# Eighteen of 64 conditioning chunks on TensorE, all of them beside w_in and w_out: a residual block on one core

## The chip, the cores and the metric

The kernel runs on one core of a Trainium2 chip. The metric is the device time of one execution in microseconds; the number for a kernel is the median of its runs. One further execution was recorded by the hardware profiler; all rows below come from it. Engines are named as the profile does: PE (TensorE), PEld (its weight loads), DVE (VectorE), ACT (ScalarE), POOL (GpSimd), SP (the queue that issues most transfers).

## The reference

One trunk layer over 256 tokens of width 2048, conditioned by a vector `c`; all in float32:

```python
mod = jax.nn.silu(c) @ w_ada[l] + b_ada[l]                     # 2048 x 12288
sh1, sc1, g1, sh2, sc2, g2 = jnp.split(mod, 6, axis=-1)
hn = rmsnorm(x) * (1.0 + sc1[:, None]) + sh1[:, None]
mix = hybrid_mixer(hn, w_in[l], ..., w_out[l])                 # 4 mLSTM heads beside 8 RG-LRU blocks
x = x + (g1[:, None] * mix).astype(x.dtype)
hn = rmsnorm(x) * (1.0 + sc2[:, None]) + sh2[:, None]
y = hier_moe(hn.reshape(B * S, D), ...)                        # 32 experts in 4 groups, 2 per token
x = x + (g2[:, None] * y).astype(x.dtype)
return rmsnorm(x) * final_g
```

The conditioning, `silu(c) @ w_ada`, is a product of one row with 96 MiB of weights. `sh1` and `sc1` are needed before `w_in`, `g1` for the first residual, `sc2` and `sh2` for the router and the experts' inputs, `g2` only where the experts' outputs are added. The router picks a group and two of its eight experts for each token.

## The kernel before, in words

All weights come in chunks of 1024 KB (128 partitions by 4 by 512 float32). SP issues the transfers in the order of the code into a ring of 7 buffers (`chunk`); a transfer waits until the chunk that had the buffer has been used. SP and PE keep the code's order, DVE and ACT are put in order by a scheduler up to the router and keep the code's order from there to the first experts (`in_order`).

**The start** (to about 140 us): the 32 chunks of `sc1` and `sh1`, on PE, with the first `w_in` chunks among them.

**Beside `w_in` and `w_out`** (to about 540 us): each of 52 chunks of `w_in` and `w_out` is split on ACT and DVE into a rounded part and a rest (`split`, lines 460 to 464, tile `ws`, three buffers of half a chunk) and multiplied on PE in three terms. After each, `between` (line 498) runs: it advances side work (gates, scores, sums) by one step and takes conditioning chunks from the generator `ada_later`. That generator has 64 chunks, 16 for each of the sections g1, sc2, sh2 and g2, in this order. A chunk goes one of two ways:

- on PE, if its number is in the set `ON_PE`: four matmuls (line 312) with the conditioning as a 32-column operand, into one PSUM tile of the section;
- on DVE else: two operations on half a chunk each (lines 320 and 322), which add to the tile `acc`.

When a section is complete, `acc_sum` (line 282) folds `acc` into the PSUM tile by four matmuls on PE, DVE adds the bias (`row`, line 289), PE turns the row into columns (line 295), and DVE writes `ada` (line 297), in `adx` too for sc2 and sh2.

`between` takes one chunk each time, and a second one at every sixth call up to the 36th. That makes 58 chunks of the 64 by the end of `w_out`. `ON_PE` holds 21 numbers, 15 of them among these 58 and the numbers 58 to 63.

**The router's wait** (about 538 to 561 us). After the last `w_out` product come the last residual (lines 782 to 784: product with the gate row `g`, addition to `X`), its transposes on PE (871), the router's product (881), and a chain of small DVE operations that ends in MS, the tokens' choices (944). PE counts them (986 to 993), DVE makes a selection matrix, and PE gathers the first round's tokens with it (970). The calls `fill(FILL[0])` and `fill(FILL[1])`, with `FILL = (4, 2)`, take four conditioning chunks behind the router's product and two behind the counting. All six are on PE.

**The experts** (to the end). Ten rounds, each with up to four experts on 32 tokens each. The chunks of the first round belong to experts 0 and 1, which need no router result (`first_weights`); they go through 13 buffers: the ring's 7, and 6 that have come free (`early`, `more`, lines 178 to 189). The later ones are addressed by the router's table `eid`. In the first round `begin` (from line 1252 on) puts the tables and one more `fill()` with `drain()` between the first chunks: there the sum of g2 is finished, and `g2_rows` spreads it.

Of the kernel before, what the change touches and what calls it, by code (L numbers as in the profile page):

```python
# [38 lines left out]
NR = len(ROUNDS)  # L39
NB = 1 + sum(n for _, n in OVER)  # L40

FILL = (4, 2)

EARLY = (2,)

BESIDE = 53


ON_PE = {0, 1, 2, 3, 5, 7, 10, 12, 14, 16, 19, 22, 32, 41, 48, 58, 59, 60, 61, 62, 63}


C_ID, C_SEL, C_LT, C_ONE, C_MASK, C_IOTA, C_SLOT = 0, 128, 176, 304, 432, 688, 817
# [54 lines left out]
def block_kernel(ctx, tc, x, c, w_ada, b_ada, w_in, b_gates, vec_a, vec_b, w_lru_a, w_lru_x, w_out,  # L107
# [20 lines left out]
    def small(shape, name):  # L128
        return st([128] + shape, name)
# [7 lines left out]
    def step():  # L137
        for q in (sums, side):
            if q:
                g = q.popleft()  # L140
                if next(g, "end") != "end":
                    q.append(g)
# [127 lines left out]
    def ada_row(sec, k):  # L270
        return chunk(w_ada[:, sec * D:sec * D + D].rearrange("(p k) (j n) -> p k j n", k=16, j=4)[:, k])
# [28 lines left out]
    def ada_later():  # L300
# [3 lines left out]
        for i, sec in enumerate((2, 4, 3, 5)):  # L304
# [3 lines left out]
            for k in range(16):  # L308
                w = ada_row(sec, k)
                if 16 * i + k in ON_PE:  # L310
                    for n in range(4):
# [184 lines left out]
    done = [0]  # L496

    def between():

        step()  # L500
        done[0] += 1
        for _ in range((done[0] < BESIDE) + (done[0] < 37 and done[0] % 6 == 0)):
            next(later, None)

    def w_in_group(col0, evac):
        ps = [pa([128, 2, S]) for _ in range(2)]
        for kk in range(4):
            by_channel(ps, kk, col0, step if col0 == 5640 else None)
            between()
        for ch in range(4):  # L510
            evac(ch, ps[ch // 2][:, ch % 2])
# [221 lines left out]
    def token_group(col0, evac):  # L733
        ps = [pa() for _ in range(2)]
        for kk in range(4):
            w = chunk(w_in[kk * 512:kk * 512 + 512, col0:col0 + 512].rearrange("(k p) n -> p k n", p=128))
            by_token(ps, w, HH, HL, kk * 4, kk == 0, kk == 3)
            between()
        for h in range(2):
            evac(h, ps[h])  # L740
# [26 lines left out]
    def w_out_chunk(ps, n, kk):  # L767
        w = chunk(w_out[kk * 512:kk * 512 + 512, n * 512:n * 512 + 512].rearrange("(k p) n -> p k n", p=128))
        Y = YM if kk < 2 else YR
        by_token(ps, w, Y[:, 0], Y[:, 1], kk % 2 * 4, kk == 2, kk == 1, step)  # L770
        between()
# [81 lines left out]
    def fill(n=1):  # L853
        for _ in range(n):
            step()
            next(later, None)
# [21 lines left out]
    for i in range(2):  # L878
        for j in range(2):
            for h in range(2):  # L880
                PE.matmul(plg[:, h], xts[i][:, j, h * 128:h * 128 + 128], wr[:, 12 + i * 2 + j], start=False,
                          stop=i == 1 and j == 1, skip_group_check=True)
    fill(FILL[0])
    for h in range(2):
        V.scalar_tensor_tensor(lg[:, h], plg[:, h], r2[:, h:h + 1], shw, op0=OP.mult, op1=OP.add)

# [104 lines left out]
        PE.matmul(pcnt[:, 0:32], ones, MS[:, h], start=h == 0, stop=h == 1)  # L991
    for h in range(2):
        PE.matmul(pcnt[:32, 32:33], MS[:, h], ones[:, 0:1], start=h == 0, stop=h == 1)
    fill(FILL[1])
    pre = small([2, 32], "pre")
    tcopy(pre, ppre)

# [333 lines left out]
```

## Time and profile before

| | us |
|---|---|
| three runs | 1353.75, 1346.56, 1346.46 |
| median of the runs | 1346.56 |
| the profiled execution, from outside | 1348.79 |
| its span in the profile | 1346.8 |
| busy in the span: PE, PEld | 1171.0, 667.1 |
| busy: DVE, ACT, POOL | 546.7, 347.9, 5.6 |

The transfers of the span are 504.81 MB, a mean of 375 GB/s. The span is what the profiler recorded between the first and the last instruction; the execution's own time is 2 us longer. Busy shares are means over stages with different limits, so they say little; what counts is read from slices and windows. A matmul's record is longer than the distance to the next one, since matmuls overlap in the array. One chunk on PE shows as eight records of line 312.

### The profile page before, as it was taken

The numbers are of one execution on the slowest core, as the hardware profiler recorded it, in microseconds if no ns is written. First come the engines' busy times: TensorE is split into PE (matmuls) and PEld (weight loads), VectorE is DVE, ScalarE is ACT, GpSimd is POOL, SyncE is SP. The second block draws the span as 40 slices with busy tenths as digits, with TensorE's granted clock in tenths as the row PEclk, the third lists the DMA queues.
The fourth block names the chain that finished last, engine by engine and source line by source line (L and its number), as shares of the span: only waits on it lengthen the run. The fifth ranks groups of instructions, "written<-read, shape, count | busy, mean of one in ns | idle before, by whom it ended". The sixth has DMA issues, their size and how long they took to land. (4 is left out here: it accounts for less than half of the span.)

```text
span 1346.8 us, 19864 instructions
## 1 busy us (share of the span) xinstructions
PE 1171.0 (87%) x8002; PEld 667.1 (50%) x8002; DVE 546.7 (41%) x987; ACT 347.9 (26%) x551; POOL 5.6 (0%) x13
## 2 busy tenths in 40 slices
PE   4898999999999999899687898878887779887885
PEld 0666889987877888443132434223341133423222
DVE  1333667779869977523013131302231013131214
ACT  2233494545445443521010011001010010101012
POOL 0000000000000000000000000000000000000000
PEclk9999999999989999899899999999998799999997
DMA  9999868689969998999999999999999999999993
GB/s 337 368 374 365 276 219 331 237 331 351 356 245 404 410 373 324 357 352 404 424 423 423 422 423 423 423 424 423 424 423 424 424 424 423 406 424 424 422 411 141
DMA packets 116896, 504.81 MB, mean 375 GB/s; under 512 B 12425, under 2 KB 14761, under 8 KB 69185
## 3 DMA queue, kind: packets, MB, share of 16 engines
q1 hardware_dynamic: 114832, 496.97, 92.5%
q0 software_dynamic: 720, 5.24, 0.9%
q8 instruction: 64, 1.05, 0.3%
q10 hardware_dynamic: 1248, 1.29, 0.3%
q14 instruction: 32, 0.25, 0.0%
HBM read 526.54 MB, written 2.10 MB: 392 GB/s over the span
## 5 line engine op out<-in xcount | busy, mean ns | idle before, releaser
L1105 PE MATMUL pa<-ring,XE 128*32 128x512 f32 x1368 | 225.8, 628 | 44.8 <-DMA ring<-in_w_e_up_dram 32.2
L463 DVE TENSOR_TENSOR ws<-ring,ws 128x1024 fp32r<-128x1024 f32 x128 | 154.9, 1221 | 64.9 <-ACT ws L462 58.5
L462 ACT ACTIVATE ws<-ring 128x1024 fp32r<-128x1024 f32 x128 | 134.7, 1060 | 164.5 <-PE pa L494 79.6
L478 PE MATMUL pa<-HH,ws 128*128 128x256 f32 x512 | 151.9, 297 | 3.6 <-ACT ws L462 1.9
L1105 PE MATMUL pa<-early,XE 128*32 128x512 f32 x656 | 135.6, 618 | 20.8 <-DMA early<-in_w_e_up_dram 12.4
L480 PE MATMUL pa<-HH,ws 128*128 128x256 f32 x512 | 149.2, 291 | 5.0 <-DVE ws L463 5.0
L479 PE MATMUL pa<-HL,ws 128*128 128x256 f32 x512 | 148.7, 290 | 1.4 <-DVE HL L373 1.4
L1105 PEld LDWEIGHTS pa<-ring,XE 128*32 128x32 f32 x1368 | 58.8, 114 | 167.9 <-issue 77.7
L1105 PE MATMUL pa<-more,XE 128*32 128x512 f32 x536 | 112.1, 616 | 15.4 <-DMA more<-in_w_e_up_dram 12.7
L1160 PE MATMUL pa<-ring,hT 128*32 128x512 f32 x640 | 108.2, 610 | 11.8 <-DMA ring<-in_w_e_down_dram 11.7
L974 ACT ACTIVATE XE<-pb,adx 128x128 f32<-128x128 f32 x80 | 36.6, 458 | 301.9 <-DVE XE L977 301.9
L478 PEld LDWEIGHTS pa<-HH,ws 128*128 128x128 f32 x512 | 102.2, 200 | 18.5 <-issue 8.4
L480 PEld LDWEIGHTS pa<-HH,ws 128*128 128x128 f32 x512 | 101.7, 199 | 6.6 <-DVE ws L463 6.6
L1137 DVE TENSOR_TENSOR hs<-hs,pa 128x512 f32<-128x512 f32 x10 | 6.9, 688 | 237.3 <-PE pa L1105 237.3
L479 PEld LDWEIGHTS pa<-HL,ws 128*128 128x128 f32 x512 | 102.1, 199 | 2.0 <-DVE HL L373 1.9
L1125 DVE TENSOR_TENSOR X<-X,pa 128x512 f32<-128x512 f32 x80 | 52.0, 684 | 116.0 <-PE pa L1123 115.9
L322 DVE SCALAR_TENSOR_TENSOR acc<-ring,cz,acc 128x1024 f32<-128x1024 f32 x78 | 98.2, 1278 | 0.4 <-DMA ring<-in_w_ada_dram 0.3
L970 PE MATMUL pb<-two,XN 128*128 128x128 f32 x640 | 77.3, 279 | 6.7 <-ACT hT L1144 6.7
L970 PEld LDWEIGHTS pb<-two,XN 128*128 128x128 f32 x640 | 73.1, 192 | 19.0 <-issue 9.2
L1105 PEld LDWEIGHTS pa<-early,XE 128*32 128x32 f32 x656 | 33.2, 113 | 83.1 <-issue 42.3
L1116 ACT ACTIVATE ys<-y 128x512 fp32r<-128x512 f32 x40 | 25.3, 632 | 181.9 <-DVE y L1114 181.9
L1160 PE MATMUL pa<-more,hT 128*32 128x512 f32 x304 | 60.7, 622 | 5.3 <-DMA more<-in_w_e_down_dram 5.3
(379 smaller groups left out, 1376.4 us busy)
## 6 DMA issues: line engine op xcount, KB each, us to landing
ring<-in_w_ada_dram SPq DMA_DIRECT2D x96, 1024.0 KB
ring<-in_w_e_gate_dram SPq DMA_DIRECT2D x62, 1024.0 KB
ring<-in_w_e_down_dram SPq DMA_DIRECT2D x61, 1024.0 KB
ring<-in_w_e_up_dram SPq DMA_DIRECT2D x57, 1024.0 KB
ring<-in_w_in_dram SPq DMA_DIRECT2D x48, 1024.0 KB
early<-in_w_e_up_dram SPq DMA_DIRECT2D x30, 1024.0 KB
more<-in_w_e_down_dram SPq DMA_DIRECT2D x29, 1024.0 KB
more<-in_w_e_up_dram SPq DMA_DIRECT2D x25, 1024.0 KB
```

The lines of the kernel that those rows point to most:

```text
L322: V.scalar_tensor_tensor(o, w[:, h:h + 2], cz[:, k, 3:4], o, op0=OP.mult, op1=OP.add)
L462: A.activation(ws[:, 0], s, AF.Copy)
L463: V.tensor_tensor(ws[:, 1], s, ws[:, 0], op=OP.subtract)
L478: PE.matmul(o, wh[:, cc], HH[:, k], start=k == 0 and ch % 2 == 0, stop=False, skip_group_check=True)
L479: PE.matmul(o, wh[:, cc], HL[:, k], start=False, stop=False, skip_group_check=True)
L480: PE.matmul(o, wl[:, cc], HH[:, k], start=False, stop=k == 15, skip_group_check=True)
L970: PE.matmul(p[:, j], XN[:, h, kk, j], which[:, h], start=h == 0, stop=h == 1)
L974: A.activation(XE[:, k], p[:, j], AF.Identity, scale=adx[:, 1, k:k + 1], bias=adx[:, 0, k:k + 1])
L1105: PE.matmul(o[c0:c0 + width], lhs(kk, j)[:, c0:c0 + width], w[:, j], start=first and j == 0, stop=last and j == 3)
L1116: A.activation(ys[0], y, AF.Copy)
L1125: V.tensor_tensor(X1[:, h, ns], X1[:, h, ns], pc, op=OP.add)
L1160: PE.matmul(pds[n][c0:c0 + width], hT[:, f, c0:c0 + width], w[:, n], start=f == 0, stop=f == 3)
```

## The change

```diff
-FILL = (4, 2)
-
-ON_PE = {0, 1, 2, 3, 5, 7, 10, 12, 14, 16, 19, 22, 32, 41, 48, 58, 59, 60, 61, 62, 63}
+ON_PE = {0, 1, 2, 3, 5, 8, 10, 13, 15, 16, 18, 20, 23, 32, 39, 48, 54, 60}
...
-        for _ in range((done[0] < BESIDE) + (done[0] < 37 and done[0] % 6 == 0)):
+        for _ in range((done[0] < BESIDE) + (done[0] < 50 and done[0] % 4 == 0)):
             next(later, None)
...
-    fill(FILL[0])
+    fill(2)
...
-    fill(FILL[1])
+    fill()
```

`between` now takes the second chunk at every fourth call up to the 48th: 52 + 12 = 64, so `ada_later` is used up by the last `w_out` chunk. Of the 64, 18 go to PE and 46 to DVE (before 21 and 43; among the 58 beside `w_in` and `w_out` 15 and 43). The calls of `fill` behind the router's product and behind the counting find no chunk and no side work left. The two lines less at the top shift every line number by two: the chunk on PE is line 310 in the changed kernel, the sum's matmuls line 280.

By groups of four `between` calls, the chunks on PE and on DVE differ in these places: the last of the RG-LRU gate's columns (4 and 0, now 4 and 1), the first k columns (2 and 2, now 3 and 2), the second v columns (0 and 4, now 1 and 4), the second o columns (1 and 4, now 0 and 5), and `w_out` in its four quarters (0 and 4, 1 and 3, 0 and 4, 0 and 4; now 1 and 4, 1 and 4, 0 and 5, 1 and 3).

On PE, from the router's transposes to the counting of the choices; before, with the four chunks of the ring between the product and the counting:

```order
L871 MATMUL pb<-cs,X_3661 128x128 x8
L881 MATMUL pa<-wr,xt 128x36 x8
L312 MATMUL pa<-ring_63,cz 32x512 x4
L312 MATMUL pa<-ring_64,cz 32x512 x4
L312 MATMUL pa<-ring_65,cz 32x512 x4
L312 MATMUL pa<-ring_66,cz 32x512 x4
L986 MATMUL pb<-MS,cs 128x32
```

and after the change, on PE from the sum of g2 to the first gather:

```order
L280 MATMUL pa<-acc,cs 32x512 x4
L293 MATMUL pb<-cs,row 128x4 x4
L869 MATMUL pb<-cs,X_3702 128x128 x8
L879 MATMUL pa<-wr,xt 128x36 x8
L984 MATMUL pb<-MS,cs 128x32
L985 MATMUL pb<-MS,cs 128x32
L986 MATMUL pb<-MS,cs 128x32
L989 MATMUL pcnt<-MS,cs 128x32 x2
L991 MATMUL pcnt<-cs,MS 32x1 x2
L968 MATMUL pb<-two,XN 128x128 x8
```

The chunks are gone from the wait, and the sum of the last section stands ahead of the router's transposes.

On DVE, the end of `w_out` and the last residual (`t` is the product with the gate, `X` the residual stream, `xt` the router's input); before:

```order
L463 TENSOR_TENSOR ws<-ring_68,ws 128x1024 x2
L322 SCALAR_TENSOR_TENSOR acc<-ring_69,cz,acc 128x1024 x2
L782 TENSOR_TENSOR t_4247<-pa,g_4202 128x512
L783 TENSOR_TENSOR X_3661<-X_3661,t_4247 128x512
L782 TENSOR_TENSOR t_4251<-pa,g_4202 128x512
L783 TENSOR_TENSOR X_3661<-X_3661,t_4251 128x512
L872 TENSOR_TENSOR xt<-pb,ada 128x512
```

and after the change:

```order
L320 SCALAR_TENSOR_TENSOR acc<-ring_68,cz,acc 128x1024 x2
L287 TENSOR_TENSOR row<-pa,brow 128x512
L780 TENSOR_TENSOR t_4283<-pa,g_4226 128x512
L295 TENSOR_SCALAR ada<-pb 128x16
L781 TENSOR_TENSOR X_3702<-X_3702,t_4283 128x512
L780 TENSOR_TENSOR t_4287<-pa,g_4226 128x512
L781 TENSOR_TENSOR X_3702<-X_3702,t_4287 128x512
L870 TENSOR_TENSOR xt<-pb,ada 128x512
```

`row`, which needs the sum's matmuls, and `ada`, which needs PE's turning of the row, stand among the operations of the residual.

On PE, in the first round of experts, where `begin` puts its tables (`eidf` and `PW`); before:

```order
L1105 MATMUL pa<-more_4560,XE 32x512 x2
L1059 MATMUL pb<-cs,eidf 1x32 x2
L1066 MATMUL pb<-cs,PW 128x128 x8
L282 MATMUL pa<-acc,cs 32x512 x4
L295 MATMUL pb<-cs,row 128x4 x4
L1105 MATMUL pa<-ring_69,XE 32x512 x2
```

and after the change:

```order
L1103 MATMUL pa<-more,XE 32x512 x2
L1103 MATMUL pa<-more_4566,XE 32x512 x2
L1057 MATMUL pb<-cs,eidf 1x32 x2
L1064 MATMUL pb<-cs,PW 128x128 x8
L1103 MATMUL pa<-ring_69,XE 32x512 x2
```

The sum is no longer there; the next expert chunk follows the tables directly.

## Rows read from the trace of the kernel before

**Rows 1.** The page, part 2: the span in 40 slices.

```profile
PE   4898999999999999899687898878887779887885
...
PEclk9999999999989999899899999999998799999997
...
GB/s 337 368 374 365 276 219 331 237 331 351 356 245 404 410 373 324 357 352 404 424 423 423 422 423 423 423 424 423 424 423 424 424 424 423 406 424 424 422 411 141
```

**Rows 2.** Windows: PE, PEld, DVE, ACT, POOL busy us, granted clock, DMA share, GB/s.

```profile
440.00:460.00 20.00, 20.00 (x96) 16.48 (x95) 19.50 (x23) 10.28 (x15) 1.05 (x2) 1.00 1.03 414
500.00:520.00 20.00, 20.00 (x106) 16.96 (x105) 17.88 (x19) 8.97 (x14) 0.00 (x0) 1.00 0.84 303
540.00:560.00 20.00, 16.93 (x116) 9.84 (x116) 10.79 (x54) 13.22 (x18) 0.00 (x0) 0.83 0.94 369
580.00:600.00 20.00, 20.00 (x180) 6.95 (x181) 3.15 (x29) 3.94 (x6) 0.00 (x0) 1.00 0.85 325
620.00:640.00 20.00, 19.11 (x140) 5.97 (x132) 11.64 (x25) 2.53 (x4) 0.00 (x0) 1.00 1.01 424
```

**Rows 3.** Timeline of SP's queue, 505 to 600 us: start, us, operation.

```profile
511.58 21.31 SPq L155 DMA_DIRECT2D ring<-in_w_ada_dram  x7
532.94 3.50 SPq L155 DMA_DIRECT2D more<-in_w_e_gate_dram  x3
...
549.10 6.22 SPq L155 DMA_DIRECT2D ring<-in_w_e_up_dram  x5
564.97 5.88 SPq L155 DMA_DIRECT2D early<-in_w_e_up_dram  x3
```

**Rows 4.** Waits of SP's queue, 500 to 640 us: us, times, longest.

```profile
SPq L155 <- PE pa L1105: 28.5, 5, 9.6
```

**Rows 5.** Timeline of PE at 175 us: start, us, operation.

```profile
175.26 1.07 PE L312 MATMUL pa<-ring,cz 128*32 128x512 f32 x8
176.25 0.39 PE L478 MATMUL pa<-HH,ws 128*128 128x256 f32 x1
```

**Rows 6.** Line 322: durations in ns (min, median, max), first and last start.

```profile
L322 DVE SCALAR_TENSOR_TENSOR acc<-ring,cz,acc x78: 1194/1279/1286, 198.5 to 533.6; 128x1024 f32<-128x1024 f32 x78
```

**Rows 7.** Timeline, end of w_out and the last residual.

```profile
538.41 0.39 PE L494 MATMUL pa<-ws,YM 128*128 128x512 f32 x1
538.96 0.69 DVE L783 TENSOR_TENSOR X<-X,t 128x512 f32<-128x512 f32 x1
...
540.28 0.69 DVE L783 TENSOR_TENSOR X<-X,t 128x512 f32<-128x512 f32 x1
```

**Rows 8.** Timeline, the sum of g2 in the first round of experts.

```profile
577.14 1.07 PE L282 MATMUL pa<-acc,cs 128*32 128x512 f32 x8
...
578.35 0.69 DVE L289 TENSOR_TENSOR row<-pa,brow 128x512 f32<-128x512 f32 x1
...
579.18 1.02 PE L295 MATMUL pb<-cs,row 128*128 128x4 f32 x8 [0.97 <-DVE row L289]
...
580.14 1.06 PE L1105 MATMUL pa<-ring,XE 128*32 128x512 f32 x8
```

**Rows 9.** Timeline, the router's wait.

```profile
545.40 6.32 PE L312 MATMUL pa<-ring,cz 128*32 128x512 f32 x32
...
550.06 0.22 DVE L944 TENSOR_TENSOR MS<-M 128x64 f32<-128x64 f32 x1
...
551.65 0.41 PE L986 MATMUL pb<-MS,cs 128*128 128x32 f32 x2
...
554.84 2.05 PE L970 MATMUL pb<-two,XN 128*128 128x128 f32 x16
```

**Rows 10.** Windows as in rows 2, around the router's wait.

```profile
540.00:544.00 4.00, 2.40 (x18) 1.96 (x18) 1.86 (x5) 3.37 (x9) 0.00 (x0) 1.00 1.00 420
544.00:548.00 4.00, 4.00 (x24) 1.96 (x27) 2.15 (x12) 4.00 (x5) 0.00 (x0) 0.50 0.84 356
552.00:556.00 4.00, 4.00 (x39) 2.56 (x39) 2.93 (x15) 0.94 (x1) 0.00 (x0) 1.00 0.92 344
```

## The prediction

> **What bounds the kernel now.** I read the slices of the span first [rows 1]. They show two regimes. From about slice 18 (610 us) nearly to the end the transfers run at 422 to 424 GB/s, slice after slice: there the weights of the experts set the pace. Before that the rate is between 219 and 410 and PE stands at nine tenths in nearly every slice from 5 to 15: from 170 to 540 us, beside `w_in` and `w_out`, PE is the bound. So the end is the moment at which transfers reach their full rate, plus a fixed number of bytes at that rate. Whatever moves that moment moves the end by as much, and nothing else that this change touches does.
>
> Second, windows of 20 us [rows 2] place that moment: 369 GB/s in 540 to 560, 325 in 580 to 600, and 424 in 620 to 640, while PE is busy for 20.00 of the 20 us from 580 and 19.11 from 620. What holds the transfers back is the third view, SP's queue [rows 3]: the conditioning chunks of the router's wait are issued up to about 532, the static experts' chunks (the ones that need no router result) from 532.9 to 555.3, and the next one only at 565, when PE gives back a first buffer. There are 13 buffers, and all are ordered by 555. From then on a transfer starts when PE has used a chunk up: SP's waits for the experts' matmuls between 500 and 640 add up to 28.5 us in 5 waits [rows 4]. So the state at which PE begins the first round (561 us) is "all 13 buffers full or nearly so", and after it PE's own speed sets the pace until the transfers have reached their full rate, at 620 at the latest. The sum below is therefore made on PE's time line up to there.
>
> **The change, part by part.** It goes against the profiled execution: 1348.8 us outside, 1346.8 of span, that is 2.2 above the median of the three runs (1346.56).
>
> 1. *Six chunks move from the router's wait into the stage of `w_in` and `w_out`.* On PE that stage had 15 chunks of its 58 and has now 18 of 64; DVE had 43 and has 46. One chunk on PE takes from 175.26 to the next matmul at 176.25, 0.99 us [rows 5]: 3 × 0.99 = +3.0 us on the engine that bounds there. One chunk on DVE is two operations of 1.279 us [rows 6], 2.56; three are 7.7 us. DVE is busy for 19.5 of 20 us at 440 to 460 but for 17.9 at 500 to 520 [rows 2]; its splits run up to two buffers ahead of PE, so I take DVE's part as hidden: 0, with 7.7 as the bad end if the cover is gone. The other end of PE's part is 0, if those 3 us fall into gaps in which PE waits anyway. The six transfers are 6.3 MB; at 303 GB/s in 500 to 520 against 424 later there is room for them.
>
> 2. *The last sum (the fold of `acc` and the row of g2) moves.* In the first round PE has the sum's matmuls at 577.14, waits for DVE's `row`, transposes it at 579.18 and goes on at 580.14 [rows 8]: those 3.0 us go. In the new order they stand between the last matmul of `w_out` and the last residual, on DVE's side too: `row` stands ahead of the first product with the gate, and `ada` ahead of the first addition to X. These are two waits that DVE did not have there; behind them on DVE stands the whole residual, and on PE, behind the transposes, the router's product, which everything up to the first gather waits for. Worked out with the same durations: the last matmul of `w_out` starts at 538.41 [rows 7], the sum's at 538.64, they take 1.07 (539.71); `row` starts 0.14 later and takes 0.69 (540.54); the transposes 0.14 later, 1.02 (541.70); `ada` then ends at about 541.9, and only then comes the first addition, which started at 538.96. Both additions shift: +2.9. So this sum costs as much before the router as it gives back in the round: 2.9 − 3.0 = −0.1. Its ends are −3.0 (if DVE's wait were covered) and +0.5.
>
> 3. *The router's wait loses its filling.* MS is ready at 550.28, the matmuls that count it start at 551.65: they stand behind four chunks, which started at 545.40 and took 6.32 us [rows 9]. Some 0.1 us of that is the hand-over, so −1.3. The other two chunks end as the first gather's operand is ready; they cost nothing and give nothing.
>
> 4. *What the filling did for PE's clock.* Four chunks should take 4 × 0.99 = 4.0 us; they took 6.32 [rows 5, 9]. The granted clock was 0.50 from 544 to 548, the lower of the two levels, after a stretch (540 to 544) in which PE was busy for 2.4 of 4 us [rows 10]; it stood at 1.00 again from 552 to 556 [rows 10], after those dense chunks, and the gather at 554.84 ran at that level, 2.05 us [rows 9]. In the changed order nothing stands on PE between the router's product and MS, nor between the counting and the gather. The clock falls as before and has nothing to raise it: the short matmuls after MS and the first gather run at 1.2 GHz. That is about +0.5 for the counting (matmuls like those of 551.65, about 1.3 us together up to the end of the counting) and +2.05 for a gather that takes twice its time. If the first gather doesn't bring the clock back, the second does the same (+2.05) and the first expert chunk loses about 1.8: +3.9 more. Which of the two it is, no row of before shows; between the ends 0 and 3.9 I take half, +2.0. From below the clock costs 0 (if it returns at once), from above 6.5.
>
> The Trainium skill, "TensorE: Matmul & The Clock Gate", section "Part 1: The HAM clock gate", says that the slow state is the default and that activity is what lifts it. By that rule the wait of the changed kernel starts and stays slow; the trace agrees with its number (0.50 after a sparse stretch, 1.00 after the chunks). By the rule alone one would put all of the 3.9 into the sum, which then comes out 1.9 higher; by the row alone, none of it.
>
> Sum: 3.0 − 0.1 − 1.3 + 0.5 + 2.05 + 2.0 = +6.2. On the profiled execution that is 1355.0; on the median of the runs 1352.7, and I say 1353.
>
> What is late next where a stall goes: with the counting 1.3 us earlier, DVE's chain from the counts to the first gather comes 1.3 earlier too, and the next thing that PE waits for is again this chain, so nothing else takes it. On SP the six transfers stand earlier in the same queue, each with the buffer seven issues back as its condition, and the experts' transfers stand directly behind the last of them.
>
> **The rivals.**
>
> *DVE becomes the bound.* Three chunks more, two of them in the third quarter of `w_out`, where ring buffers, splits and residuals share DVE. For it: 19.5 of 20 us at 440 to 460 [rows 2]. Against it: PE was busy for all of those 20 us (20.00) beside the DVE that was that full, and DVE's load falls to 17.9 at 500 to 520. If all of it shows: 6.2 + 7.7, some 1360.5.
>
> *The weights come sooner.* Without conditioning in the wait, the experts' chunks follow `w_out` directly, 6 × 1.05 MB / 424 GB/s = 14.8 us sooner, and in a kernel that ends transfer-bound this would move the end. 1352.7 − 14.8 = 1338, faster than before. It decides if the experts' matmuls of the first round wait for transfers; from the point at which all 13 buffers are full before PE begins (561 us), every earlier arrival is worth nothing. Against it: they are ordered by 555.3, and SP's queue waits for PE there, not PE for it [rows 3, 4]. The Trainium skill, "Perfetto Trace Analysis", section "Optimization Strategy", says that kernels with regimes of different limits may gain from interleaving them, which is this rival's case; the trace doesn't bear it out here, with 325 GB/s at 580 to 600, after both regimes have met.
>
> *Nothing measurable.* The change trades the same work about: PE's three chunks fall into gaps, the clock comes back with the first gather or isn't lost. 0 − 0.1 − 1.3 + 0.5 + 2.05 is 1.1 up: 1347.7. For it: PE's clock also dips for short times in other slices of the stage [rows 1], which can move by some us with any shift.
>
> **How the numbers follow.** My forecast (1349 to 1357) 0.60, nothing measurable 0.20, DVE the bound 0.13, weights sooner 0.07. The range leaves out most of "weights sooner" and the end of "DVE": 1344 to 1362. A measurement of this kernel can tell about 1% from no change, 13.5 us. Slower by more than that is above 1360: the upper half of the DVE case and a little of the forecast, 0.10. Faster is below 1333, only with the whole of the 14.8 and a stage that absorbs its chunks: 0.02. The rest, 0.88, is the same.
>
> **What the changed profile would show.** Right: line 310 (the chunk on PE) has 144 records instead of 168, all before the last residual; the stage up to the last matmul of `w_out` ends some 3 us later than 538.4; the first addition of the last residual starts 3.5 us after that matmul instead of 0.5; the granted clock is at 0.50 from the router's product to at least the end of the first gather, which takes about 4 us; the counting starts within 0.2 us of MS; between the transposes of the tables and the next expert chunk there is no gap of 3 us; SP orders the 13th buffer before the first round begins, and rates from 620 on are 424 again. Wrong: if PE waits for DVE's splits in `w_out` (the DVE rival), if rates in the first round rise towards 424 (weights sooner), or if the gather takes 2.05 us (no clock lost).

## The result, and the profile after

The changed kernel takes 1367.43 us (median of 4 runs, 1366.92 to 1369.98) against 1350.04 for the kernel before (4 runs, 1346.46 to 1353.75): ratio 1.0126, 95% interval 1.0093 to 1.0159. I had said 1353.0 and a range of 1344 to 1362; it is slower than the range allows. The times of the kernel before fall in two groups, near 1346.5 and near 1354, and its profiled execution (1348.79) belongs to the lower one, from which I had reckoned; all four times of the changed kernel lie above both. The profiled execution of the changed kernel takes 1366.92, span 1364.5, that is 17.7 of span more than before.

The slices of the page after, which answer to [rows 1]:

```profile
PE   4888999999998999799777998968987688887886
...
PEclk9998999999998999699988999999999899999998
...
GB/s 336 381 378 361 263 231 283 341 326 380 302 313 409 400 344 227 247 298 393 424 424 423 423 422 423 423 423 424 423 423 424 424 424 420 410 424 423 423 411 148
```

Two differences ahead of slice 19 bear on the result (single slices from 5 to 11 move too, up and down). The rate falls to 227 to 298 in slices 15 to 17, and the lowest clock of a slice stands in slice 16, the router's wait. Full rate comes about 20 us later: 389 GB/s in 620 to 640 where [rows 2] had 424, and 424 from 640. After that the rates of the slices stay within 4 GB/s of those before, but for the last one. So the frame of the prediction holds: the end moved by as much as the start of the round.

Where the 17.7 us arise is read on TensorE's time line (two rows of DVE stand among it). Two marks divide it: the last matmul of `w_out`, and the first expert chunk out of the ring in the first round (580.14 before [rows 8]).

```profile
551.26 0.39 PE L492 MATMUL pa<-ws,YM 128*128 128x512 f32 x1
551.58 1.07 PE L280 MATMUL pa<-acc,cs 128*32 128x512 f32 x8
553.53 1.06 PE L293 MATMUL pb<-cs,row 128*128 128x4 f32 x8 [0.88 <-DVE row L287]
554.72 0.68 DVE L781 TENSOR_TENSOR X<-X,t 128x512 f32<-128x512 f32 x1
555.54 0.30 PE L869 MATMUL pb<-cs,X 128*128 128x128 f32 x1 [0.96 <-DVE X L781]
556.78 1.76 PE L869 MATMUL pb<-cs,X 128*128 128x128 f32 x7 [0.93 <-DVE X L781]
558.47 3.63 PE L879 MATMUL pa<-wr,xt 128*128 128x36 f32 x16
566.68 0.22 DVE L942 TENSOR_TENSOR MS<-M 128x64 f32<-128x64 f32 x1
567.05 0.61 PE L984 MATMUL pb<-MS,cs 128*128 128x32 f32 x2 [4.96 <-DVE MS L942]
...
570.49 3.92 PE L968 MATMUL pb<-two,XN 128*128 128x128 f32 x16 [0.81 <-DVE two L959]
...
577.47 3.78 PE L968 MATMUL pb<-two,XN 128*128 128x128 f32 x16
581.18 4.69 PE L1103 MATMUL pa<-early,XE 128*32 128x512 f32 x32
...
597.05 1.09 PE L1064 MATMUL pb<-cs,PW 128*128 128x128 f32 x8
598.07 3.64 PE L1103 MATMUL pa<-ring,XE 128*32 128x512 f32 x32
```

The first mark moves from 538.41 [rows 7] to 551.26, +12.85. The way between the marks grows from 41.7 to 46.8, +5.1. All of the small steps of the prediction (sum, counting, clock in the wait) lie in the second part, where I had +3.2. The miss is the first part, where I had +3.0.

The stage itself, from the first split with conditioning beside it to the first mark (one window each, before and then after; columns as in [rows 2]):

```profile
160.43:538.41 377.98, 372.50 (x2283) 315.03 (x2282) 298.20 (x392) 199.49 (x295) 4.36 (x7) 0.98 0.86 325
```

```profile
158.88:551.26 392.38, 380.84 (x2308) 316.73 (x2307) 304.53 (x397) 198.38 (x295) 4.34 (x7) 0.97 0.84 318
...
420.00:440.00 20.00, 14.07 (x51) 10.40 (x50) 20.00 (x27) 8.83 (x15) 1.05 (x2) 0.83 1.04 405
460.00:480.00 20.00, 19.98 (x95) 15.35 (x94) 12.71 (x15) 4.90 (x6) 0.00 (x0) 0.91 1.02 394
464.00:468.00 4.00, 4.00 (x21) 3.69 (x20) 2.39 (x6) 0.00 (x0) 0.00 (x0) 0.91 1.03 392
468.00:472.00 4.00, 4.00 (x13) 3.19 (x12) 3.46 (x3) 0.93 (x1) 0.00 (x0) 0.66 1.02 361
520.00:540.00 20.00, 17.33 (x84) 13.28 (x83) 11.98 (x13) 7.97 (x13) 0.00 (x0) 0.91 0.42 149
```

It is 14.4 us longer (and began 1.6 earlier, from the stretch ahead of it). TensorE without work: 392.38 − 380.84 = 11.5 against 5.5, that is +6.1. Low clock: (1 − granted clock) × length, added up over windows of 20 us, is 6.8 before and 12.2 after, +5.4. The three windows of 20 us shown make 7.0 of it, and the kernel before has 1.00 in each of them; elsewhere it gives back 1.6. Of the 7.0, 3.4 and 1.8 stand behind the two waits told below (420 to 440, 520 to 540). The 1.8 of 460 to 480 has no wait in front of it: TensorE's records leave hardly a gap there (19.98 of 20 us), and the level falls behind the third section's sum, whose last piece is 16 short records on a few columns each.

```profile
463.68 2.92 PE L293 MATMUL pb<-cs,row 128*128 128x4 f32 x16
```

What is left is +2.9, about three chunks at 0.99. The split is not sharp: some of the low clock lies in time in which TensorE stood still anyway. By windows of 1 us, with busy time alone counted, the clock makes +4.0, and then 4.3 is left. So the term I gave (+3.0) fits what is left, and beside it stand 10 to 11.5 us that I had put at nothing.

The largest wait is at the end of the last group of `w_in`. First the kernel before (ACT and PE), then after (ACT, DVE, PE):

```profile
428.46 1.06 ACT L462 ACTIVATE ws<-ring 128x1024 fp32r<-128x1024 f32 x1 [1.66 <-PE pa L494]
429.54 1.28 ACT L751 ACT_TABLE_LOAD   x1
430.83 1.09 ACT L751 ACTIVATE TO<-pa 128x512 f32<-128x512 f32 x2
431.81 2.56 ACT L755 ACTIVATE YR<-XG 128x256 fp32r<-128x256 f32 x8
...
434.17 0.50 PE L493 MATMUL pa<-ws,YR 128*128 128x512 f32 x1 [1.38 <-DVE YR L756]
```

```profile
429.13 1.28 ACT L749 ACTIVATE TO<-pa 128x512 f32<-128x512 f32 x2 [5.70 <-PE pa L492]
430.30 2.55 ACT L753 ACTIVATE YR<-XG 128x256 fp32r<-128x256 f32 x8
432.76 2.94 ACT L460 ACTIVATE ws<-ring 128x1024 fp32r<-128x1024 f32 x3
...
425.49 4.87 DVE L320 SCALAR_TENSOR_TENSOR acc<-ring,cz,acc 128x1024 f32<-128x1024 f32 x4
430.27 1.29 DVE L647 SCALAR_TENSOR_TENSOR TO<-TO,XG 128x512 f32<-128x512 f32 x2
431.48 2.77 DVE L754 TENSOR_TENSOR YR<-XG,YR 128x256 fp32r<-128x256 f32 x8
...
433.85 0.80 PE L490 MATMUL pa<-ws,YR 128*128 128x512 f32 x1 [4.08 <-ACT ws L460]
436.63 0.79 PE L492 MATMUL pa<-ws,YR 128*128 128x512 f32 x1 [1.56 <-DVE ws L461]
```

Before, ACT makes the split of the next `w_out` chunk (428.46) and only then the tanh, which must wait for TensorE's last matmul of the group; TensorE goes on with that split. After, tanh and YR stand ahead of that split. ACT stands still for 5.70 us in front of the tanh, and TensorE then for 4.08 until tanh, YR and split are done. ACT's and DVE's order is the scheduler's there, not the kernel's. Read from the built programs, the tanh stands behind the splits of 37 calls before the change and of 36 after it, and the residual of the third quarter behind those of 49 and of 48. At the residual of the second quarter the order turned as well (45 and 44), without a wait on TensorE there. The second place with a wait is the residual of the third quarter, on DVE: the matmul at 523.97 waits 2.67 us (shown at the end) for a split that stands behind that residual.

```profile
520.27 1.31 DVE L780 TENSOR_TENSOR t<-pa,g 128x512 f32<-128x512 f32 x2 [1.05 <-PE pa L492]
522.69 3.49 DVE L461 TENSOR_TENSOR ws<-ring,ws 128x1024 fp32r<-128x1024 f32 x3
```

### The profile page after: what moved, and what is told of

Its sections match the earlier page's. It is cut to its first block, busy times and chain, and to the rows that moved or that the text cites. A ratio compares the mean times of both kernels' runs of the same rounds, so it can differ in the third digit from the quotient of the medians.

```text
span 1364.5 us, 19828 instructions
## 1 busy us (share of the span) xinstructions
PE 1180.3 (86%) x7978; PEld 677.2 (50%) x7978; DVE 552.7 (41%) x993; ACT 346.1 (25%) x551; POOL 5.6 (0%) x13
## 5 line engine op out<-in xcount | busy, mean ns | idle before, releaser
L1103 PE MATMUL pa<-ring,XE 128*32 128x512 f32 x1368 | 221.5, 617 | 46.7 <-DMA ring<-in_w_e_up_dram 33.3
L1103 PE MATMUL pa<-early,XE 128*32 128x512 f32 x656 | 134.6, 621 | 19.6 <-DMA early<-in_w_e_up_dram 12.5
L1158 PE MATMUL pa<-ring,hT 128*32 128x512 f32 x640 | 114.6, 624 | 12.2 <-DMA ring<-in_w_e_down_dram 12.1
L320 DVE SCALAR_TENSOR_TENSOR acc<-ring,cz,acc 128x1024 f32<-128x1024 f32 x84 | 105.0, 1275 | 0.2 <-DMA ring<-in_w_ada_dram 0.2
L968 PE MATMUL pb<-two,XN 128*128 128x128 f32 x640 | 80.9, 286 | 7.5 <-ACT hT L1142 6.7
L968 PEld LDWEIGHTS pb<-two,XN 128*128 128x128 f32 x640 | 76.4, 199 | 19.1 <-issue 9.3
L1103 PEld LDWEIGHTS pa<-more,XE 128*32 128x32 f32 x536 | 28.9, 113 | 69.0 <-issue 32.6
```

What stands on the lines that cost most here:

```text
L320: V.scalar_tensor_tensor(o, w[:, h:h + 2], cz[:, k, 3:4], o, op0=OP.mult, op1=OP.add)
L968: PE.matmul(p[:, j], XN[:, h, kk, j], which[:, h], start=h == 0, stop=h == 1)
L1103: PE.matmul(o[c0:c0 + width], lhs(kk, j)[:, c0:c0 + width], w[:, j], start=first and j == 0, stop=last and j == 3)
L1158: PE.matmul(pds[n][c0:c0 + width], hT[:, f, c0:c0 + width], w[:, n], start=f == 0, stop=f == 3)
```

## The experiments

All times in us. The stage is the stretch above, "idle" TensorE without work in it, "to ring" the way between the two marks (all three from the profiled execution, one for each run). The profiled execution took 1372.57 in x3 and 1357.44 in x13, 6.2 above and 3.1 below their medians, so their stages do not go with the medians beside them.

| run | median | ratio to before, interval | stage | idle | to ring |
|---|---|---|---|---|---|
| before | 1347.0 to 1354.1, beside the runs | | 378.0 | 5.5 | 41.7 |
| the change | 1367.43 | 1.0126, 1.0093 to 1.0159 | 392.4 | 11.5 | 46.8 |
| x1_wait_alone | 1350.75 | 1.0032, 1.0002 to 1.0061 | 378.1 | 5.5 | 44.8 |
| x2_warm | 1368.93 | 1.0148, 1.0105 to 1.0192 | 392.2 | 11.5 | 47.8 |
| x3_doubles_pe | 1366.34 | 1.0121, 1.0077 to 1.0165 | 395.3 | 11.2 | 46.9 |
| x4_sum_in_wait | 1365.24 | 1.0124, 1.0081 to 1.0167 | 392.2 | 11.5 | 44.6 |
| x5_split_first | 1367.01 | 1.0121, 1.0075 to 1.0166 | 392.0 | 10.8 | 46.8 |
| x6_warm_groups | 1361.49 | 1.0086, 1.0062 to 1.0110 | 392.2 | 11.5 | 41.2 |
| x7_early_pairs | 1369.09 | 1.0134, 1.0085 to 1.0184 | 397.5 | 16.7 | 44.7 |
| x8_three | 1359.39 | 1.0052, 1.0027 to 1.0076 | 392.4 | 10.8 | 39.0 |
| x9_swap | 1362.19 | 1.0086, 1.0058 to 1.0113 | 386.3 | 8.0 | 46.3 |
| x10_light | 1393.74 | 1.0302, 1.0256 to 1.0348 | 393.9 | 12.3 | |
| x11_light_first | 1393.80 | 1.0302, 1.0256 to 1.0348 | 391.3 | 10.4 | |
| x12_best | 1354.08 | 1.0029, 1.0005 to 1.0052 | 386.1 | 8.0 | 40.7 |
| x13_sum_cover | 1360.53 | 1.0075, 1.0046 to 1.0104 | 392.3 | 10.2 | 39.0 |
| x14_fewer | 1363.71 | 1.0097, 1.0063 to 1.0132 | 395.4 | 12.5 | 39.0 |

### x1_wait_alone: the second half of the change by itself

```diff
-                if k == 15:
+                if k == (9 if i == 3 else 15):
...
+                if i == 3 and k == 9:
+                    return
```

> This is the kernel before with its last six chunks of conditioning left out altogether (the last section is summed over 10 of its 16 rows, so its gate values are not the reference's); the stage of w_in and w_out keeps its 58 chunks as they were, nothing stands in the router's wait, and the last sum stands ahead of the last residual. It is the second half of the change alone. If the recorded steps 2 to 4 hold (sum moved -0.1, counting -1.3, clock +4.55): 3.2 us above the kernel before, ratio about 1.002. By the steps as they can be read from the trace after (first addition +2.9, product of the router +0.9, counting -1.2, then +0.6, -0.4, +1.9, +0.65, +1.7, +1.05 by the lower clock, round -3.0): 5.1 above, ratio about 1.004. Rival, that the whole loss comes from the empty wait and the 12.9 us within w_out are scatter between two executions: 17 above, ratio 1.013.

Measured: +0.32%, 4.3 us on 1347, and between the marks 44.8 − 41.7 = +3.1. The stage is that of the kernel before to 0.2 us. So the empty wait is not what costs 17 us; the stage is.

### x2_warm and x6_warm_groups: the clock in the wait

```diff
...
     fill(2)
+    pd = pa((128, 504))
+    for i in range(10):
+        PE.matmul(pd[:32], cz[:, i, 3:35], wr512, start=True, stop=True)
...
```

In x6 the output is `pd[i % 4 * 32:i % 4 * 32 + 32]`. Behind the counting stand three more such matmuls in x2 and four in x6.

> The changed kernel with ten matmuls of 504 columns on data at hand, into a psum tile that nobody reads, behind the router's product, and three more behind the counting. They load nothing and only keep TensorE at work. If the clock is what the empty wait costs, the low stretch from 556 ends by about 565, the gathers take 2.05 us and the first expert chunk 3.64: 5 to 6 us below the changed kernel (about 1361.5). If the clock rises as late as without them, 0 to 0.5 above it.

Missed by its form: into one column group the ten matmuls run one behind the other and hold up the counting.

```profile
562.19 10.76 PE L886 MATMUL pa<-wr,cz 128*32 128x504 f32 x20
572.87 0.41 PE L989 MATMUL pb<-MS,cs 128*128 128x32 f32 x2
```

> The changed kernel with ten matmuls of 504 columns spread over the four column groups, as a chunk's are, behind the router's product and four behind the counting, on data at hand and into a psum tile nobody reads. The first try put all into one column group and held up the counting by 6.0 us (566.85 to 572.87) while it gave back 5 to 6 by the higher clock. If the clock is what the empty wait costs, MS is counted at once, the first expert chunk starts 6.5 us after the first gather instead of 10.7 and the next members 5.6 after that instead of 6.6: 5 us below the changed kernel, 1362. If the clock needs what the chunks' transfers bring as well, no change.

```profile
561.47 4.79 PE L855 MATMUL pa<-wr,cz 128*32 128x504 f32 x20
566.50 0.38 PE L992 MATMUL pb<-MS,cs 128*128 128x32 f32 x2 [0.25 <-DVE MS L950]
...
569.30 2.39 PE L976 MATMUL pb<-two,XN 128*128 128x128 f32 x16 [0.44 <-DVE two L967]
...
576.10 3.64 PE L1112 MATMUL pa<-early,XE 128*32 128x512 f32 x32
```

Spread over four column groups the same twenty records take 4.79 instead of 10.76. The counting starts with MS, and the gather takes 2.39 and the first expert chunk 3.64 instead of 3.92 and 4.69. Between the marks 46.8 becomes 41.2, and the whole falls by 5.9. The clock of the empty wait is worth 5.6 to 5.9 us.

```profile
560.00:580.00 20.00, 12.82 (x60) 12.08 (x61) 10.29 (x56) 9.46 (x10) 0.00 (x0) 0.50 0.53 222
```

```profile
560.00:580.00 20.00, 17.71 (x125) 9.75 (x125) 13.11 (x71) 11.54 (x15) 0.00 (x0) 0.86 0.50 207
```

The granted clock over 560 to 580 is 0.50 in the changed kernel (first row) and 0.86 in x6 (second); nothing but work on TensorE was added. The Trainium skill, "TensorE: Matmul & The Clock Gate", section "Part 1: The HAM clock gate", says that the slow state is the default and activity releases it; these two rows agree.

### x4_sum_in_wait: the last sum

```diff
-    drain()
+    while side:
+        g = side.popleft()
+        if next(g, "end") != "end":
+            side.append(g)
...
-    fill(2)
+    acc_sum()
...
-    fill()
+    step()
+    step()
```

> The changed kernel with the last sum taken apart: its matmuls behind the router's product, the row's addition on VectorE while TensorE counts, the transposes in the first round. The first addition to X then stands 0.5 us behind the last matmul of w_out again (2.9 earlier) and the round pays 1.0 for the transposes: 1.9 below the changed kernel. If the eight records of the sum also bring the clock back early, up to 6 below. Rival, that the addition of the row delays the first gather as much as it frees the residual: no change.

Measured: 2.2 below the changed kernel, and 2.2 between the marks (46.8 to 44.6). The totals alone would not carry it (the ratios are 1.0124 and 1.0126); the way between the marks does. The sum in front of the residual costs what step 2 said. It did not bring the clock back: its eight records took 1.94 us and the gather behind them still 3.91.

### x3_doubles_pe and x5_split_first: order or work alone

The first edit is x3's. In x5 the next chunk is issued, and split, ahead of `between()` at calls 36 and 48 (the other pieces):

```diff
-ON_PE = {0, 1, 2, 3, 5, 8, 10, 13, 15, 16, 18, 20, 23, 32, 39, 48, 54, 60}
+ON_PE = {0, 1, 2, 3, 5, 8, 10, 13, 15, 16, 18, 20, 23, 32, 39, 44, 48, 54, 59, 60}
...
             by_token(ps, w, HH, HL, kk * 4, kk == 0, kk == 3)
+            if ahead and kk == 3:
+                ahead()
             between()
...
+        if (n, kk) == (2, 1):
+            hold(3, 2, 2)
         between()
```

> The changed kernel with two chunks more on TensorE, 44 and 59: the second ones of the two calls that put two chunks in a row on VectorE, right ahead of the YR splits and of the residual of the third quarter. If VectorE's order at these two places makes the loss (waits of 4.1, 1.6 and 2.7 us on TensorE and the low clock behind them), 6 to 9 us below the changed kernel (1358 to 1361) with TensorE's own 2.0 taken off. If the stage is bound by TensorE's work, as recorded: 2.0 above it (1369). If the transfers bind there: no change.

> The changed kernel with the same chunks on the same engines in the same calls; only at two places the first split of the next w_out chunk is written ahead of the conditioning chunks of that call (its transfer two places earlier in SP's queue), so that ACT and DVE have the split of call 37 ahead of the last tanh and YR again, and DVE has that of call 49 ahead of the residual of the third quarter, as in the kernel before. Theory 'order of the splits': TensorE's waits there go (4.1, 1.6 and 2.7 us in the changed kernel, 1.4 in the kernel before) and with them the low clock behind them (6.8 and 3.4 us at half, worth 5.1): 9 to 12 us below the changed kernel, 1355.5 to 1358.5. Theory 'VectorE has too much work' (the recorded rival): the waits come back at other places, at most 3 below it. Theory 'transfers are too many for the stage': no change.

Both missed. In x3 (one chunk of each of the two calls moved to TensorE) the order stays turned (36 and 48): the tanh still stands ahead of the split on ACT, and TensorE still waits 3.08 and 1.62 us there and 2.70 at the residual. In x5 the order is that of the kernel before at these two places (37 and 49); the residual's wait falls from 2.67 to 0.88 and 0.53, but at YR one wait took the place of another:

```profile
429.80 0.50 PE L496 MATMUL pa<-ws,YR 128*128 128x512 f32 x1 [1.14 <-ACT YR L761]
433.61 2.77 DVE L762 TENSOR_TENSOR YR<-XG,YR 128x256 fp32r<-128x256 f32 x8
434.08 0.80 PE L497 MATMUL pa<-ws,YR 128*128 128x512 f32 x1 [3.78 <-DVE YR L762]
```

DVE came to YR only at 433.61, behind the two chunks (43, 44) that this call gives it. So the order alone does not give the time back: at YR the work that DVE has in this call counts as well.

### x9_swap, x10_light, x11_light_first: both together

x9 is x5 with the first edit, 18 chunks on TensorE still. x10 is the changed kernel, and x11 is x5, with the second.

```diff
-ON_PE = {0, 1, 2, 3, 5, 8, 10, 13, 15, 16, 18, 20, 23, 32, 39, 48, 54, 60}
+ON_PE = {0, 1, 2, 3, 5, 8, 10, 13, 15, 16, 18, 20, 23, 32, 39, 43, 44, 60}
...
+                    cols = 8 if 16 * i + k in (42, 43, 44, 58, 59) else 512
...
-                        o = acc[:, h:h + 2]
+                        o = acc[:, h:h + 2, :cols]
```

> As the run with the splits first, and 43 and 44 on TensorE in place of 48 and 54: 18 chunks there as in the changed kernel, but none on VectorE in the call ahead of YR (5.1 us of VectorE gone from that call), and TensorE busy with two chunks while ACT does tanh and YR. Theory 'VectorE is behind at call 36 and the splits' order does the rest' (both are needed): TensorE's waits from 429 to 437 (4.9 us with the splits first alone, 5.6 in the changed kernel) fall to 1.5 or less and the low clock from 432 (6.8 us at half) goes: 6 to 8 us below the changed kernel, 1359.5 to 1361.5. Theory 'transfers are too many for the stage': no change, since none of them moves.

> The changed kernel, but VectorE adds only 8 of every 512 columns of the chunks 42, 43, 44, 58 and 59 (so the last two sections' conditioning is not the reference's); transfers, order of the splits and TensorE's work stay. VectorE has 12 us less to do. Theory 'VectorE's work alone': the waits at 434 and 524 go, 9 to 11 us below the changed kernel (1356 to 1358). Theory 'both are needed': on ACT the split still stands behind tanh and YR, so about 4 us of waiting at 434 and the low clock behind it stay; only the 2.7 at 524 and its 1.7 may go: 0 to 5 below (1362 to 1367).

> As x10, with the splits written first as in the run before: VectorE light and the order as in the kernel before. Theory 'both are needed': all waits of w_out go, as does the low clock at 432 and 525: 9 to 12 us below the changed kernel (1355.5 to 1358.5). Theory 'transfers are too many': no change here either.

x9 gained 5.2, a little under its forecast, with the same number of chunks on each engine and the same transfers, so transfers too many for the stage are not the cause of these 5.2. It takes both chunks of call 36 off DVE, beside the order. All waits from 429 to 437 are gone, and with them the low clock:

```profile
420.00:440.00 20.00, 19.71 (x94) 14.55 (x94) 17.84 (x25) 10.02 (x16) 1.05 (x2) 1.00 1.02 405
```

x10 and x11 compute another router shift, so other experts follow and their total says nothing here; their stage does. In x10, with 10 us of DVE's work gone (busy 294.6 of the stage, 304.5 after the change), the two waits that stand behind the order are as long or longer:

```profile
435.44 0.79 PE L491 MATMUL pa<-ws,YR 128*128 128x512 f32 x1 [4.08 <-ACT ws L461]
...
526.64 0.70 PE L491 MATMUL pa<-ws,YR 128*128 128x512 f32 x1 [3.69 <-ACT ws L461]
...
522.37 1.30 DVE L781 TENSOR_TENSOR t<-pa,g 128x512 f32<-128x512 f32 x2 [5.25 <-PE pa L493]
```

The last row shows it best: DVE has nothing to do for 5.25 us, in front of a residual that waits for TensorE, while the split that TensorE needs next stands behind it. At YR neither edit is enough by itself: the order alone leaves 1.14 and 3.78 (x5), the lighter DVE alone 4.08 (x10). With both edits (x11) the waits at YR are 1.13 and 0.66 instead of 4.08 and 1.56. The whole stage of x11 is only 1 us shorter than the changed kernel's, though: the lighter DVE has another residual (the second quarter's) ahead of a split, with a new wait of 2.66 at 484. So its "all waits of `w_out` go" was wrong, and DVE's amount of work alone does not set the stage. That both together remove the waits at YR is shown by x9 and x11.

### x7_early_pairs: the double calls elsewhere

```diff
-ON_PE = {0, 1, 2, 3, 5, 8, 10, 13, 15, 16, 18, 20, 23, 32, 39, 48, 54, 60}
+ON_PE = {0, 2, 4, 6, 9, 10, 12, 15, 18, 21, 22, 24, 26, 29, 31, 40, 47, 54}
...
-        for _ in range((done[0] < BESIDE) + (done[0] < 50 and done[0] % 4 == 0)):
+        for _ in range((done[0] < BESIDE) + (done[0] in (1, 2, 3, 4, 5, 6, 7, 8, 9, 10, 11, 12))):
```

> The changed kernel with all twelve double calls among the first twelve (18 chunks on TensorE still, on the calls where the kernel before has them and three more), which leaves ACT's and DVE's order at calls 37, 44, 46 and 50 as in the kernel before. Theory 'order of the splits': the stage of w_out runs as before and the whole pays TensorE's three chunks and the empty wait, 3 + 5: 1353 to 1358. Theory 'VectorE has too much work': the 24 chunks beside the first twelve calls stop TensorE there by several us, 1360 and above.

Missed by the first theory, as the second had it (1360 and above). The late order was that of the kernel before (37 and 49), so the placing of the late chunks turns it and not their number. From the last tanh to the first mark the run took only 1.4 us more than that kernel. But the stage was 16 us late by then, with waits of 1.3 to 1.9 us for splits from 203 to 280 and one of 6.79 for a sum's row at 339. Twelve pairs in a row have no free place in the early calls, and DVE's work can stop TensorE where it is crowded.

### x8_three and x12_best: the mends together

x8 is x5, x4's sum and six plus four matmuls for the clock; x12 has x9's chunks in place of x5's.

> The changed kernel with all three mends: the splits first (9 to 12), the last sum's matmuls in the router's wait and its row beside the counting (about 2), and six plus four matmuls on data at hand to keep the clock up (about 5). If the three add up: 16 to 19 below the changed kernel, 1348 to 1351, that is the kernel before with TensorE's three chunks more. If one stands in for another (the sum's matmuls already bring the clock back, or the scatter hides them): 1354.

> x9's splits and chunks, the last sum in the router's wait and ten matmuls on data at hand to keep the clock. From the run with three mends (1359.4): another 6 to 8 us less, 1351.5 to 1353.5, and not below the kernel before (1346.6 to 1354).

x8 came out at 1359.4, 8 to 11 above its forecast since x5 gave nothing; the two mends in the wait add up (46.8 to 39.0). x12 came out at 1354.1, just above its forecast, 13.3 below the changed kernel, and 0.3% above the kernel before. No run beats the kernel before.

### x13_sum_cover and x14_fewer: what is left of the stage

From x12's set to x13's, and from there to x14's:

```diff
-ON_PE = {0, 1, 2, 3, 5, 8, 10, 13, 15, 16, 18, 20, 23, 32, 39, 43, 44, 60}
+ON_PE = {0, 1, 2, 3, 5, 8, 10, 13, 15, 16, 18, 20, 32, 43, 44, 48, 49, 50}
+ON_PE = {0, 1, 2, 3, 5, 8, 10, 13, 15, 18, 43, 44, 48, 49, 50}
```

> The run with all mends (1354.1), with 49 and 50 on TensorE beside 48, in place of 39, 60 and 23: still 18 chunks there. TensorE then has chunks of its own around the third section's sum, and VectorE's first write into acc after that sum comes later, so that it does not stand 5.2 us in front of it. Theory 'the sum at call 40': the waits of 1.4 and 0.4 us and the low clock from 461 (6.8 us at half) go: 4 to 5 below that run, 1349 to 1350. Theory 'the number of chunks': no change.

> As x13 with 16, 20 and 32 on VectorE: 15 chunks on TensorE in the stage, as in the kernel before, and 49 on VectorE. Recorded step 1 says that a chunk costs TensorE 0.99 us and VectorE nothing where it has room: 3 below x13. If VectorE has no room left in the scores and values part (calls 14 to 29), its 7.7 us come back as waits: 0 to 8 above x13.

x13 missed: the waits at the sum shrank (0.84 instead of 1.44 and 0.38), but the clock fell there all the same, and longer waits came at 492 and 528 (1.39 instead of 0.86, and 1.88 instead of 0.88 and 0.53); it is 6.4 slower than x12. Which of the moved chunks makes these waits was not run. x14 took three chunks off TensorE, and the stage grew by 3.1: idle +2.3, low clock +1.6 (13.8 to 15.4), DVE's busy time 303.8 to 311.4. The rest fell by 0.7, where three chunks at 0.99 would make 3.0. The totals of x13 and x14 overlap (1357.4 to 1364.2, 1359.0 to 1365.0), and the stages are one execution each, so this speaks against three more chunks hidden on DVE but does not settle it. What the other 8 us of x12's stage (386.1 against 378.0) consist of is told by its window:

```profile
159.83:545.93 386.10, 378.10 (x2308) 314.31 (x2306) 304.71 (x398) 198.28 (x295) 4.34 (x7) 0.98 0.85 323
```

Idle time is 2.5 of it (8.0 against 5.5); by 20-us windows as above the clock is another 1.8, and the rest, 3.8, is put down to work, the three chunks foremost (not shown by a run of its own). Whether some other placing of 64 chunks would do without them stays open.

## Why the prediction was wrong

*Frame (the start of the round moves the end):* right. The first expert chunk out of the ring moved by 17.9, the span by 17.7.

*Step 1, the step that failed.* Its TensorE part, +3.0, fits what is left over (2.9 to 4.3). What failed is "its splits run up to two buffers ahead of PE, so I take DVE's part as hidden: 0". The cover was there in the windows I read (20.00 of 20 us on TensorE beside a DVE at 19.50), but it rested on two things. The split for TensorE's next chunk stood ahead of the operation that waits for TensorE's last matmul of a group (tanh, residual), and DVE came to YR in time. After the change the scheduler has that order turned at calls 36 and 48, and both chunks of call 36 (43 and 44) are DVE's; the kernel before had two there as well, but the second (41) on TensorE. By what rule the scheduler turns the order is not shown: with 44 on TensorE (x3) it stays turned, with one chunk in each of these calls (x7) it does not. At YR both count: restoring the order alone (x5) or lightening DVE alone (x10) leaves the waits, both together (x9, x11) remove them or most of them. At the residual the order does most of it (2.67 becomes 0.88 and 0.53 in x5, 3.69 in x10). Measured: +6.1 of waits in the stage. And behind the two new waits TensorE ran at the lower level for 6.8 and 3.4 us, 5.1 of the +5.4, for which the sum had no term. Even my bad end (7.7) was too small for that reason.

*Step 2, the last sum:* right in its two terms, one term short. The first addition comes 3.46 behind the last matmul instead of 0.55 (554.72 against 551.26; [rows 7]), and the sum's 3.0 us of [rows 8] are gone from the round: the ring's chunk starts 1.02 behind L1064. What it lacked: behind the sum and its wait (0.88) the granted clock is 0.51 from 556 to 560 already, and the router's product, from the last addition's start to its end, takes 6.1 instead of 5.2.

*Step 3, the counting:* right. It starts 0.37 behind the start of MS (566.68) instead of 1.59 [rows 9], −1.2.

*Step 4, the clock in the wait:* mechanism right, size too small by about 1. I took 4.55 of at most 6.5; x6 gives 5.6 to 5.9. The first gather did not bring the clock back, nor did the second (3.92 and 3.78), and the first expert chunk ran partly low as well (4.69 for 3.64): together 2.8 of the 3.9 of which I had taken half (2.0). In x1 the second gather (3.24) and the chunk (4.05) were partly at the higher level already, and the way between the marks came out at +3.1.

*Rivals.* "DVE becomes the bound" (0.13) came nearest in place, with "PE waits for DVE's splits in `w_out`" as its sign, and was half right: DVE's total work is not the lever (x10 takes 10 us of it away and the waits stay, x9 keeps it and they go), but what DVE has to do in call 36 is one of the two causes at YR, and crowded early it stops TensorE (x7). Its price, all 7.7, was below the measured loss. It put two of DVE's three chunks more into the third quarter of `w_out`; DVE has one more there (5 for 4), and one more in the second `o` columns, where call 36 is. "The weights come sooner": no; rates at 620 to 640 fell. "Nothing measurable": no.

## What to carry to other kernels

Where an engine's operands are prepared by others a buffer or two ahead, full busy time does not prove the cover: look in the preparing engines' queues for an operation that waits for the bound engine and stands ahead of its next operand. An edit that only moves side work can turn that order where a scheduler sets it, so compare the order at group ends (evacuations against the next split), and what the preparing engine has to do just there, before pricing a part at nothing. And price a new wait on TensorE above its length: here the low clock cost 3.4 behind waits of 4.08 and 1.56 us and 1.7 behind one of 2.67, some 0.6 of their length. Shorter ones, such as the 1.08 at 255 us, had no low stretch behind them.

## What was not expected of the hardware

Ten 504-column matmuls with 32 output partitions took 10.76 us in one column group (x2) and 4.79 in four (x6). The Trainium skill, "TensorE: Matmul & The Clock Gate", section "Why this matters for your kernels", gives 2.38 times for three small matmuls of 512 columns in distinct groups. The ratio here is 2.2 for four groups in float32, and x2's ten ran partly at the higher clock.

A wait of 2.67 us, in a stage in which TensorE is otherwise busy nearly throughout, was followed by the lower level (524 to 528 at 0.67). And behind the third section's sum the level fell with hardly a gap in TensorE's records (0.91 in 464 to 468, 0.66 in 468 to 472, shown above). The rows of the wait:

```profile
523.97 0.50 PE L492 MATMUL pa<-ws,YR 128*128 128x512 f32 x1 [2.67 <-DVE ws L461]
```

```profile
520.00:524.00 4.00, 1.33 (x7) 0.79 (x5) 3.73 (x6) 1.79 (x5) 0.00 (x0) 1.00 0.95 364
524.00:528.00 4.00, 4.00 (x12) 3.19 (x13) 2.18 (x2) 0.99 (x2) 0.00 (x0) 0.67 0.70 219
```
